# First-layer rotation tables of an S5 mixer made per quarter and kept on chip, with a new order of steps, in a two-layer hybrid decoder trunk

## The chip, the core and the metric

The kernel runs on one core of a Trainium2 chip. A core has a matrix engine (PE), a vector engine (DVE), an activation engine (ACT), a small general engine (POOL) and a queue engine (SP); each works through its own instructions in order, and they wait for each other through semaphores. Copies between the chip's memory (SBUF) and DRAM are DMAs, which SP, ACT or POOL issue. The metric is the device time of one execution in microseconds (us), as the median of several runs.

## The reference

Two layers; each has a mixer and a feed-forward part. What the change touches is the S5 group inside the mixer, cut here to its core:

```python
h = x * (1.0 + scale1) + shift1
u, q, k, v = jnp.split(h @ w_in[l], [D_SSM, D_SSM + D_ATT, D_SSM + 2 * D_ATT], axis=-1)
# s5_mixer(u): 32 groups of 16 channels, each drives 64 complex states
delta = jnp.exp(log_step)[:, None]
mag, ang = jnp.exp(lam_re * delta), lam_im * delta
lb_re, lb_im = mag * jnp.cos(ang), mag * jnp.sin(ang)
bu_re, bu_im = jnp.einsum('blgc,gpc->blgp', u32, bb_re), jnp.einsum('blgc,gpc->blgp', u32, bb_im)
# s_t = (lb_re + i lb_im) * s_{t-1} + bu_t, by associative_scan over 512 tokens
y = Re(C s) + d_skip * u32
y = gelu(y); y = y * sigmoid(y @ glu_w + glu_b)
att = diff_attention(rotary(q), rotary(k), v)      # 4 heads, 2 softmax maps each
mix = concat([y, att]) @ w_out[l]
x = layer_norm(ALPHA * x + (1 + gate1) * mix)
x = layer_norm(ALPHA * x + (1 + gate2) * ffn(x))   # SwiGLU, 1024 -> 2816 -> 1024
```

## The kernel before

Every large matmul is done three times on numbers split in two: `mm3` multiplies high by high, high by low and low by high part. So each unit of weights (128 x 1024 numbers, `wunit`) is loaded by SP into `wraw`, its high part `whi` is copied by ACT, and its low part `wlo` is subtracted on DVE. PE's matmuls of a unit wait for both.

**The first layer's mixer** is where everything has to be made while the first matmuls run. In order of PE's work: the S5 input projection (`ups`) and the values (`vps`) with the modulation columns being reduced on DVE (`mraw`: one 128 x 1024 load and one instruction each); then the projections to q and k of four heads (`qkps`), 96 matmuls a head, into which the S5 steps, the attention steps (`sps`, `po`) and more `mraw` columns are woven; then the S5 gate (`glups`) and the output projection (`ops`). After that comes the feed-forward part (`gps`, `dps`).

**S5 in chunks of 8 tokens, in four quarters** `q` of 8 groups each. For the layer, `s5_params` makes powers of the state's factor (`pw`) and the angle of 8 steps, split in two parts (`hi`, `lo`), in five parts on POOL or DVE (`OPT["par"]` says which part is on DVE). For each quarter:

- `s5_build`: tables `Gt` and `QT` (each six 128 x 512 instructions on DVE), the kernel inside a chunk `kps` (PE), copied by ACT to `ksb`, finished by DVE and written by a DMA to DRAM (`kd`), from where eight POOL DMAs bring it back in Toeplitz form (`M`); `QT` is transposed on PE (`qps`) to `Q`.
- `s5_rot`: cosine and sine of k times the angle, k = 0 to 63: eleven DVE instructions on 128 x 256, and two sines on ACT. Written to DRAM (`sC`) by two DMAs, later loaded back to `csl` by SP in `inp`.
- `inp`, `inT`, `scan`, `sout`: the quarter's inputs are transposed (`utp`), multiplied by `Q` (`vps` of line 589), rotated by the tables (`rp`), scanned along the chunks, rotated back, and multiplied by `M` and `Gt` (`yps`).

**Buffers.** `thl`, `cs`, `ns`, `ksb`, `ta`, `btmp`, `dt`, `gl` and others take turns in two buffers of one ring, `t5`. An instruction that writes a buffer waits until whatever used it two turns ago is over; for a buffer that a DMA reads, until that DMA has landed.

**What sets the order.** Each engine's instructions are put in a fixed order when the kernel is built. The hints come from a string per step of the first stage (`START`: `p` the next part of `s5_params`, `r` of the rope tables, `v` a unit for the values, `V` matmuls of it, `A` two `mraw` columns, `b` a build step) and from `PLAN`: due times, counted in steps of the projections, for the kinds `bld` (build), `s5`, `att`, `mod` (`mraw`), `pf` (weight unit) and `cs` (`s5_rot` of the next quarter).

Of the kernel before, what the change touches and what calls it, by code (L numbers as in the profile page):

```python
# [14 lines left out]
ALU = mybir.AluOpType  # L15
# [4 lines left out]
START = ['', '', '', 'v', 'ppvV', 'rpV', 'ApvvA', 'VAVVb']  # L20
LAG, LAG1 = 2, 1
PLAN = ({'bld': [1.264, 2.8128, 2.8128, 7.5302, 15.0069, 15.7908, 16.6324, 22.2347, 24.025, 24.025, 24.025, 31.5693, 31.8037, 32.6247, 36.6694, 39.8654, 39.8664, 44.4181, 55.2875, 55.2875], 's5': [2.4963, 13.7411167, 15.82, 17.6903, 17.9768, 17.9768, 28.1555, 32.3101, 33.8664, 33.8664, 41.8348, 41.8348, 41.8348, 44.9401, 56.3771, 61.9808, 63.9276, 74.4357, 74.4357, 74.9633], 'att': [32.6299, 32.6299, 32.6299, 34.4688, 34.4688, 37.9126, 37.9126, 37.9126, 38.4369, 42.2702, 48.2563, 48.2563, 48.2563, 48.2563, 53.3008, 55.2114, 55.2114, 55.2114, 62.4974, 64.6963, 65.1666, 65.1666, 66.8965, 69.8788, 69.8788, 69.8788, 69.8788, 69.8788, 72.9166, 73.1266492, 78.0578164, 79.4594, 84.4816, 84.4816, 84.4816, 84.4816, 84.4816, 85.7045, 86.611, 86.611, 86.611, 87.1372, 87.1372, 87.1372, 87.1372, 87.1372, 87.1372, 87.1372, 87.1372, 87.1372, 87.7613, 88.3711, 92.1141, 94.0138, 95.5657, 99.9], 'mod': [10.9986, 18.0979, 25.5229, 28.8809, 38.8480964, 39.702, 45.7126, 48.3167, 48.3167, 49.5891, 50.7771, 51.8893, 59.3159, 62.6235, 62.6235, 62.6235, 65.1638, 68.4286, 78.3464, 89.495], 'pf': [15.904, 15.9839, 26.2995, 26.2995, 39.217, 46.2033, 61.5805, 61.9828, 61.9828, 77.3237, 84.6088, 88.9481, 89.2859, 89.9011], 'cs': [2.3738, 2.3738, 3.9308, 15.3106]}, {'s5': [0, 9.5668, 14.1521, 22.5905, 23.0853, 23.0853, 28.7962, 33.7987, 53.4804, 53.9093, 54.6366, 54.6366, 54.6366, 54.89, 57.9461, 62.766, 63.1181, 64.2437, 76.6993, 79.0981], 'att': [32.001, 32.001001, 32.001001, 32.001001, 32.001001, 36.2691, 36.9654, 49.5504, 49.5634, 49.946, 52.2004, 52.2014, 52.2014, 53.123, 53.4199, 53.4634231, 53.4644231, 54.3593, 56.3216, 58.3250688, 61.5574297, 61.5584297, 62.6277, 62.6277, 64.4714996, 64.4715006, 64.4715016, 64.4715026, 64.4715036, 64.4715046, 64.4715056, 64.4715066, 64.4715076, 64.4715086, 64.4715096, 64.4715106, 64.4715116, 64.4715126, 82.7565, 82.7565, 82.7566, 82.7566, 83.9079, 87.4356, 87.4366, 87.4376, 90.018, 91.9921, 91.9931, 91.9941, 91.9951, 91.9951, 91.9951, 91.9951, 91.9951, 99.9], 'pf': [1.9638689, 9.1450603, 14.6524633, 14.6534633, 19.9457, 32.098, 37.9847, 48.098, 51.1731991, 74.7986995, 74.7986995, 81.1276, 84.5849, 86.8909]})
OPT = {'par': [0, 0, 1, 0, 0], 'MODQ': 'sync', 'q_bld': 1, 'q_s5': 0, 'q_att': 0, 'q_pf': 0, 'CSQ': 'scalar', 'plo': [[1, 0, 1, 0, 0, 0, 0, 0, 0, 0, 0, 1, 0, 0, 0, 0, 0, 0], [0, 0, 0, 0, 0, 0, 0, 1, 1, 0, 0, 0, 0, 1, 0, 0, 0, 0]]}
# [3 lines left out]
P = 128  # L27
# [35 lines left out]
def trunk_kernel(tc, xT, x, c, pos, modw, modb, wst, s5a, s5bc, s5d, glub, lamv, subw, lng, lnr, out):  # L63
    nc = tc.nc
    from contextlib import ExitStack

    with ExitStack() as es:
# [355 lines left out]
        def s5_build(l, q, pm):  # L423
# [54 lines left out]
            ksb = t5([P, P], name="ksb")  # L478
# [27 lines left out]
        def s5_rot(l, q, pm):  # L506
# [9 lines left out]
            cs = t5([P, 2, 4, 64], name="cs")  # L516
# [9 lines left out]

            ns = t5([P, 256], name="ns")
            ts(ns, flat(st), -1.0, ALU.mult)
            eng = getattr(nc, "gpsimd" if l else OPT["CSQ"])
            eng.dma_start(sC[q][:, 256:768], cs.rearrange("p r g k -> p (r g k)"))  # L530
            eng.dma_start(sC[q][:, 0:256], ns)
# [118 lines left out]
        def s5_gen(l, u2, us, yh, yl):  # L650
# [3 lines left out]
            def inp(q):  # L654
                if l:
                    Q[q] = s5_load_q(l, q, us[0][:, 0:1] if q == 0 else src)
                U[q] = s5_in(u2, q)
                C[q] = sm([P, 768], "csl", 1)
                nc.sync.dma_start(C[q], sC[q])
# [22 lines left out]
            seq = [(fn, (q,)) for q in range(4) for fn in (inp, inT, scan, sout)]  # L682
            seq += [(yT, (b, ih)) for b in range(2) for ih in range(2)]
# [259 lines left out]
        for l in range(L):  # L943
# [7 lines left out]
            if l == 0:  # L951
# [18 lines left out]
                rots = list(range(4))  # L970
# [16 lines left out]
                with queued(marks(), (POOL,)), strict():  # L987
# [5 lines left out]
                    for k in range(NK):  # L993
# [11 lines left out]
                        for c_ in START[k]:  # L1005
# [4 lines left out]
                            elif c_ == "c":  # L1010
                                s5_rot(0, rots.pop(0), pms[0])
                            elif c_ == "p":
                                next(par, None)
                            elif c_ == "r":
                                next(rope, None)
                            elif c_ == "b":
                                next(bld)
                            else:
                                mods_bg(cols, 2, "A2")
# [36 lines left out]
            def tick():  # L1056
                while plan and plan[0][0] < now[0] + 1:
# [10 lines left out]
                    elif kind == "cs":  # L1068
                        with queued(marks() if OPT["q_bld"] else m0, (POOL,)):
                            if rots:  # L1070
                                s5_rot(0, rots.pop(0), pms[0])
# [315 lines left out]
```

## Time and profile before

| | |
|---|---|
| time of the runs | median 1258.78 us of 3 (1256.43 to 1260.86) |
| the profiled execution | 1254.48 us, its span 1252.7 us |
| PE busy | 1186.2 us, 95% of the span |
| DVE busy | 813.6 us, 65% |
| ACT busy | 481.9 us, 38% |
| POOL busy | 162.3 us, 13% |

The span runs from the first to the last instruction; the 1.8 us around it are the same launch. Busy shares are averages over stages: after the first layer's mixer PE is busy nearly all the time, so what happens before that is what can be won or lost here.

### The profile page before, as it was taken

How to read it: one execution, taken by the hardware profiler on the slowest of the kernel's cores; microseconds unless marked ns; L12 is line 12 of the kernel's file. 1: busy time of each engine (PE TensorE's matmuls, PEld its weight loads, DVE VectorE, ACT ScalarE, POOL GpSimd, SP SyncE). 2: the span in 40 equal slices, each digit the busy share in tenths (PEclk: the TensorE clock that was granted, in tenths of full speed). 3: DMA queues.
4: the chain of work that ended last, by engine and by line, in shares of the span. 5: the costliest groups of instructions: out<-in, count | busy, mean ns of one | idle time of the engine just before them, and what ended most of it. 6: DMA issues, size and time to landing. Idle time of an engine off the chain costs nothing.

```text
span 1252.7 us, 17629 instructions
## 1 busy us (share of the span) xinstructions
PE 1186.2 (95%) x6736; PEld 988.7 (79%) x6736; DVE 813.6 (65%) x1505; ACT 481.9 (38%) x848; POOL 162.3 (13%) x289
## 2 busy tenths in 40 slices
PE   4898788999999999999999999999999999999997
PEld 3687676779888888888877788877988888888885
DVE  6779798786787675798558366757665222244556
ACT  3436255536222222343446355553623222234330
POOL 8921230010000010000001243000000000000001
PEclk9899789999999999999999999999999999999999
DMA  9784535535577577645334663223463333333241
GB/s 351 270 209 125 105 84 167 176 128 166 187 256 270 178 234 192 199 157 166 102 98 144 195 178 102 72 97 102 158 192 97 93 100 101 97 89 117 68 134 68
DMA packets 60469, 188.68 MB, mean 151 GB/s; under 512 B 8065, under 2 KB 13985, under 8 KB 60385
## 3 DMA queue, kind: packets, MB, share of 16 engines
q1 hardware_dynamic: 51408, 170.94, 43.0%
q0 software_dynamic: 5088, 13.42, 4.1%
q10 hardware_dynamic: 3888, 3.20, 1.0%
q8 instruction: 53, 0.87, 0.3%
q14 instruction: 32, 0.25, 0.1%
HBM read 172.90 MB, written 12.53 MB: 148 GB/s over the span
## 4 chain that ended last, share of the span: by engine, by line
PE 73%; DVE 11%; POOL 6%; DMA 4%; issue 4%; ACT 2%; DVEq 0%; POOLq 0%; ACTq 0%
PE gps L116 39%; PE dps L116 18%; PE ops L116 4%; PE qkps L116 2%; PE vps L116 2%; POOL s5tmp L104 1%; PE ups L116 1%; DVE wlo L104 1%; DMA wraw<-in_wst 1%; PE glups L116 1%; PE po L116 1%; DVE mraw L110 1%; DVE x L107 1%; PE sps L757 1%; DMA kd<-ksb 1%
## 5 line engine op out<-in xcount | busy, mean ns | idle before, releaser
L104 DVE TENSOR_TENSOR wlo<-wraw,whi 128x1024 fp32r<-128x1024 f32 x180 | 219.6, 1222 | 262.8 <-ACT whi L113 262.1
L113 ACT ACTIVATE whi<-wraw 128x1024 fp32r<-128x1024 f32 x184 | 194.2, 1057 | 390.3 <-PE gps L116 249.8
L116 PE MATMUL gps<-hT2h,whi 128*128 128x512 f32 (+1 forms) x768 | 286.5, 373 | 0.6 <-DVE rtmp L104 0.4
L116 PE MATMUL gps<-hT2l,whi 128*128 128x512 f32 (+1 forms) x768 | 285.8, 372 | 0.0
L116 PE MATMUL gps<-hT2h,wlo 128*128 128x512 f32 (+1 forms) x768 | 285.4, 372 | 0.0
L116 PE MATMUL dps<-whi,ah 128*128 128x512 f32 x704 | 219.6, 391 | 0.0
L116 PEld LDWEIGHTS gps<-hT2h,whi 128*128 128x128 f32 x768 | 144.7, 188 | 26.0 <-DVE rtmp L104 0.9
L116 PEld LDWEIGHTS gps<-hT2l,whi 128*128 128x128 f32 x768 | 144.7, 188 | 24.9
L116 PEld LDWEIGHTS gps<-hT2h,wlo 128*128 128x128 f32 x768 | 144.7, 188 | 24.9
L116 PEld LDWEIGHTS dps<-whi,ah 128*128 128x128 f32 x704 | 132.2, 188 | 28.6 <-DVE rtmp L104 1.2
L116 PE MATMUL dps<-wlo,ah 128*128 128x512 f32 x352 | 137.1, 390 | 0.0
L110 DVE SCALAR_TENSOR_TENSOR mraw<-mraw,scb 128x1024 f32<-128x1024 f32 x96 | 114.2, 1219 | 5.4 <-DMA mraw<-in_modw 5.4
L113 ACT ACTIVATE ah<-aT 128x512 fp32r<-128x512 f32 x88 | 53.6, 626 | 91.2 <-PE dps L116 72.8
L104 DVE TENSOR_TENSOR ah<-aT,ah 128x512 fp32r<-128x512 f32 x88 | 59.3, 688 | 41.3 <-ACT ah L113 41.1
L116 PEld LDWEIGHTS dps<-wlo,ah 128*128 128x128 f32 x352 | 66.1, 188 | 13.4
L116 PE MATMUL ops<-whi,am 128*128 128x512 f32 x128 | 43.1, 398 | 0.0
L761 ACT ACTIVATE e<-sps,nm 128x128 f32<-128x128 f32 (+3 forms) x64 | 33.3, 525 | 19.3 <-DVE nm L759 18.7
L554 POOL DMA_DIRECT2D M<-kd x64 | 33.8, 535 | 41.0 <-DMA kd<-ksb 37.9
L116 PE MATMUL qkps<-wlo,hTh 128*128 128x256 f32 x128 | 38.1, 298 | 0.5 <-DVE wlo L104 0.5
L116 PE MATMUL qkps<-whi,hTh 128*128 128x256 f32 x128 | 37.9, 298 | 0.0
L116 PE MATMUL qkps<-whi,hTl 128*128 128x256 f32 x128 | 37.9, 297 | 0.0
L116 PE MATMUL qkps<-whi,hTnh 128*128 128x256 f32 x128 | 37.4, 293 | 0.0
(285 smaller groups left out, 1858.9 us busy)
## 6 DMA issues: line engine op xcount, KB each, us to landing
wraw<-in_wst SPq DMA_DIRECT2D x184, 512.0 KB, 3.7
mraw<-in_modw SPq DMA_DIRECT2D x96, 512.0 KB, 5.1
M<-kd POOLq DMA_DIRECT2D x64, 64.0 KB, 4.4
gb<-in_lnr SPq DMA_DIRECT2D x8, 512.0 KB, 3.9
csl<-sC SPq DMA_DIRECT2D x8, 384.0 KB, 3.7
xT<-in_xT SPq DMA_DIRECT2D x8, 256.0 KB, 6.7
x<-in_x SPq DMA_DIRECT2D x4, 512.0 KB, 4.6
G<-gd SPq DMA_DIRECT2D x4, 512.0 KB, 4.8
```

The lines of the kernel that those rows point to most:

```text
L104: (eng or nc.vector).tensor_tensor(out, a, b, op=op)
L107: nc.vector.scalar_tensor_tensor(out, a, s, b, op0=op0, op1=op1)
L110: nc.vector.scalar_tensor_tensor(out, a, s, b, op0=ALU.mult, op1=ALU.mult, accum_out=acc_out)
L113: nc.scalar.activation(out, in_, AF.Copy, scale=scale)
L116: nc.tensor.matmul(ps, a, b, start=start, stop=stop)
L554: nc.gpsimd.dma_start(M[16 * j : 16 * j + 16], ksrc)
L757: nc.tensor.matmul(ps[:, m, c_], qT[rows, i * P : (i + 1) * P], kT[rows, c_], start=False, stop=c_.stop == n)
L761: nc.scalar.activation(e[:, m, :n], ps[:, m, :n], AF.Exp, bias=nm[:, m : m + 1], accum_out=ss[:, i, m : m + 1])
```

## The change

The rotation tables of the first layer are no longer written to DRAM and read back. `s5_rot` makes them into a tile `tri` of one buffer, which `scan` reads; the next quarter's tables are made after the scan that read the last ones. `ksb` gets a buffer of its own too. In the second layer the tables still go through DRAM, with one DMA in place of two. `START` and `PLAN` have new entries, kind `cs` is gone, and part 3 of `s5_params` (five small instructions: the cosine's two, and three for the power of 8 of the magnitude, `r8`) is on DVE in place of POOL.

```diff
-START = ['', '', '', 'v', 'ppvV', 'rpV', 'ApvvA', 'VAVVb']
+START = ['', '', '', 'v', 'pvrpVp', '', 'pVVAvv', 'AAVbV']
...
-            ksb = t5([P, P], name="ksb")
+            ksb = sm([P, P], "ksb", 1)
...
-            cs = t5([P, 2, 4, 64], name="cs")
+
+            tri = sm([P, 768], "tri", 1)
+            cs = tri[:, 256:].rearrange("p (r g k) -> p r g k", r=2, g=4)
...
-            ns = t5([P, 256], name="ns")
-            ts(ns, flat(st), -1.0, ALU.mult)
-            eng = getattr(nc, "gpsimd" if l else OPT["CSQ"])
-            eng.dma_start(sC[q][:, 256:768], cs.rearrange("p r g k -> p (r g k)"))
-            eng.dma_start(sC[q][:, 0:256], ns)
+            ts(tri[:, 0:256], flat(st), -1.0, ALU.mult)
+            if l:
+                nc.gpsimd.dma_start(sC[q], tri)
+            return tri
...
-                C[q] = sm([P, 768], "csl", 1)
-                nc.sync.dma_start(C[q], sC[q])
+                if l:
+                    C[q] = sm([P, 768], "tri", 1)
+                    nc.sync.dma_start(C[q], sC[q])
+
+            def rot(q):
+                C[q] = s5_rot(0, q, pms[0])
...
             seq = [(fn, (q,)) for q in range(4) for fn in (inp, inT, scan, sout)]
+            if l == 0:
+
+                seq = [(rot, (0,))] + [(fn, (q + (fn is rot),)) for q in range(4) for fn in (inp, inT, scan, rot, sout)
+                                       if fn is not rot or q < 3]
```

How the instructions move, at three places. The names are tiles of the program; a number in a name is the buffer's.

**ACT, end of the first stage.** Before: `whi_357` is the high part of a unit for the values, `s5tmp` the sine of the S5 angle, `xT_330` the input of the seventh and eighth step.

```order
L113 ACTIVATE whi_326<-wraw_324 128x1024
L370 ACT_TABLE_LOAD
L370 ACTIVATE s5tmp_143<-s5tmp_143 128x16
L371 ACTIVATE s5tmp_143<-s5tmp_143 128x16
L113 ACTIVATE whi_357<-wraw_355 128x1024
L980 ACTIVATE xT_330<-xT_330,mods_114 128x512
```

After: the same unit is `whi_355`.

```order
L113 ACTIVATE whi_326<-wraw_324 128x1024
L113 ACTIVATE whi_355<-wraw_353 128x1024
L226 ACT_TABLE_LOAD
L226 ACTIVATE rcos_121<-rang_152 128x32
L227 ACTIVATE rsin_122<-rang_152 128x32
L370 ACTIVATE s5tmp_143<-s5tmp_143 128x16
L371 ACTIVATE s5tmp_143<-s5tmp_143 128x16
L987 ACTIVATE xT_330<-xT_330,mods_114 128x512
```

The unit's high part now stands ahead of the sines and of the table load that they need.

**DVE, the third quarter's `QT`.** Before, `ksb` is followed by the `QT` table, whose temporaries `ta` take turns with `ksb` in the ring.

```order
L107 SCALAR_TENSOR_TENSOR ksb<-mask_86,s5dt,ksb 128x16
L104 TENSOR_TENSOR QT<-pw,s5bc 128x512
L104 TENSOR_TENSOR ta<-pw,s5bc 128x512
L104 TENSOR_TENSOR QT<-pw,s5bc 128x512
L104 TENSOR_TENSOR QT<-QT,ta 128x512
L104 TENSOR_TENSOR ta<-pw,s5bc 128x512
L110 SCALAR_TENSOR_TENSOR mraw,mods<-mraw,scb 128x1024
L104 TENSOR_TENSOR QT<-QT,ta 128x512
L107 SCALAR_TENSOR_TENSOR gl<-gl,yps 128x512
```

After:

```order
L107 SCALAR_TENSOR_TENSOR ksb<-mask_86,s5dt,ksb 128x16
L104 TENSOR_TENSOR QT<-pw,s5bc 128x512
L104 TENSOR_TENSOR ta<-pw,s5bc 128x512
L104 TENSOR_TENSOR QT<-pw,s5bc 128x512
L104 TENSOR_TENSOR QT<-QT,ta 128x512
L104 TENSOR_TENSOR ta<-pw,s5bc 128x512
L772 RECIPROCAL rho<-ss 128x1 x2
L104 TENSOR_TENSOR QT<-QT,ta 128x512
```

The order is nearly the same; what differs is that `ksb` is no longer in the ring that `ta` takes its buffer from.

**PE, the first head's projection.** Here only the change is shown: after 24 of the head's 96 matmuls (`qkps`; `hTh_135` belongs to the second of its two weight units) come the first quarter's transposes and products and the second quarter's `kps`. Before, the head's 96 matmuls and 23 of the next ran without them.

```order
L116 MATMUL qkps<-whi,hTh_135 128x256 x2
L495 MATMUL qps<-ident,QT 128x128 x4
L575 MATMUL utp<-ident,UU 128x128 x4
L495 MATMUL qps<-ident,QT 128x128 x4
L589 MATMUL vps<-UU,Q 64x64 x16
L476 MATMUL kps<-Gt,s5bc 32x112 x8
L476 MATMUL kps<-s5bc 32x16 x8
L116 MATMUL qkps<-wlo,hTh_135 128x256
```

And DVE between that head's two weight units: the second one's low part (the last row) follows the first quarter's `QT`, two `mraw` columns, the second quarter's whole `Gt` (its last rows here) and the first quarter's first rotation (`rp`, `wz`).

```order
L104 TENSOR_TENSOR Gt<-pw,s5bc 128x4x128
L104 TENSOR_TENSOR s5bc<-btmp 128x64 x2
L104 TENSOR_TENSOR ta<-pw,s5bc 128x512
L445 COPY s5bc<-s5bc 64x8x16 x2
L104 TENSOR_TENSOR Gt<-Gt,ta 128x4x128
L104 TENSOR_TENSOR Gt<-pw,s5bc 128x4x128
L104 TENSOR_TENSOR ta<-pw,s5bc 128x512
L104 TENSOR_TENSOR rp<-vps,tri 128x1024
L104 TENSOR_TENSOR Gt<-Gt,ta 128x4x128
L104 TENSOR_TENSOR wz<-rp 128x512
L104 TENSOR_TENSOR wlo<-wraw,whi 128x1024 x2
```

Before, eleven instructions of the second `s5_rot` and the lambda's small ones stood between the two units.

## Rows read from the trace of the kernel before

**Rows 1.** Stretches: us, busy PE, PEld, DVE, ACT, POOL; PEclk, DMA share, GB/s.

```profile
62.60:101.00 38.40, 34.97 (x265) 31.39 (x264) 30.59 (x73) 15.15 (x25) 10.22 (x19) 1.00 0.85 211
101.00:149.00 48.00, 37.06 (x391) 31.51 (x391) 46.74 (x102) 22.36 (x51) 11.20 (x18) 0.86 0.41 100
157.00:215.00 58.00, 47.60 (x444) 39.52 (x443) 52.39 (x118) 30.03 (x80) 11.12 (x23) 0.91 0.44 127
270.00:1252.70 982.70, 964.66 (x5147) 804.45 (x5146) 596.84 (x1055) 362.95 (x598) 71.72 (x126) 1.00 0.45 142
```

**Rows 2.** The same view, three stretches at half of the granted clock.

```profile
44.40:51.20 6.80, 6.08 (x14) 4.85 (x15) 5.00 (x8) 4.53 (x8) 6.35 (x13) 0.51 0.87 310
133.20:146.80 13.60, 10.27 (x102) 8.58 (x103) 13.23 (x31) 3.79 (x7) 3.00 (x5) 0.50 0.21 7
160.50:167.30 6.80, 5.74 (x28) 5.77 (x28) 5.16 (x13) 3.78 (x9) 1.16 (x4) 0.50 0.43 115
```

**Rows 3.** What PE waited for, 14 to 215 us: total, times, longest.

```profile
PE qps L495 <- DVE QT L104: 5.6, 2, 3.9
PE qps L495 <- DVE gl L107: 4.5, 1, 4.5
PE vps L116 <- ACT whi L113: 4.1, 1, 4.1
```

**Rows 4.** What DVE waited for, 60 to 215 us.

```profile
DVE ksb L107 <- ACT ksb L113: 2.0, 2, 1.8
DVE thl L104 <- DMA sC<-ns: 1.0, 1, 1.0
```

**Rows 5.** ACT in order of time: start, us, instruction, idle before and releaser.

```profile
37.48 1.28 ACT L370 ACT_TABLE_LOAD   x1
43.80 0.21 ACT L370 ACTIVATE s5tmp<-s5tmp 128x16 f32<-128x16 f32 x1 [5.04 <-POOL s5tmp L101]
44.03 1.04 ACT L113 ACTIVATE whi<-wraw 128x1024 fp32r<-128x1024 f32 x1
```

**Rows 6.** DMAs that SP issued from 36.7 to 36.85 us: to landing.

```profile
wraw<-in_wst SPq DMA_DIRECT2D x1, 512.0 KB, 3.9
```

**Rows 7.** POOL in order of time, while DVE works and after.

```profile
52.72 2.22 POOL L104 TENSOR_TENSOR pt<-pw 128x16 f32<-128x16 f32 x2
58.80 0.45 POOL L104 TENSOR_TENSOR pt<-pw 128x32 f32<-128x32 f32 x2
```

**Rows 8.** DVE in order of time.

```profile
62.63 0.31 DVE L104 TENSOR_TENSOR btmp<-s5bc,kre 128x128 f32<-128x128 f32 x1 [4.03 <-POOL pw L104]
67.83 0.41 DVE L104 TENSOR_TENSOR thl<-kio,phihi 128x256 f32<-128x256 f32 x1
75.67 0.43 DVE L104 TENSOR_TENSOR thl<-kio,phihi 128x256 f32<-128x256 f32 x1
156.41 0.69 DVE L104 TENSOR_TENSOR ta<-pw,s5bc 128x512 f32<-128x512 f32 x1 [7.15 <-DMA kd<-ksb]
157.02 1.22 DVE L110 SCALAR_TENSOR_TENSOR mraw<-mraw,scb 128x1024 f32<-128x1024 f32 x1
```

**Rows 9.** DMAs issued from 140.9 to 157 us: count, size, us to landing.

```profile
mraw<-in_modw SPq DMA_DIRECT2D x1, 512.0 KB, 10.9
csl<-sC SPq DMA_DIRECT2D x1, 384.0 KB, 10.0
kd<-ksb ACTq DMA_DIRECT2D x1, 64.0 KB, 9.5
gd<-mods POOLq DMA_DIRECT2D x1, 4.0 KB
```

**Rows 10.** The chain that ended last, in order of time: start, us, count.

```profile
75.23 0.88 PE qkps L116 x7
```

**Rows 11.** ACT in order of time, a change from one function to another.

```profile
106.04 1.28 ACT L226 ACT_TABLE_LOAD   x1
107.34 0.42 ACT L226 ACTIVATE cs<-thl 128x256 f32<-128x256 f32 x1
```

More of the change, by code (lines that the diff above doesn't have):

```diff
@@ L23 @@
-OPT = {'par': [0, 0, 1, 0, 0], 'MODQ': 'sync', 'q_bld': 1, 'q_s5': 0, 'q_att': 0, 'q_pf': 0, 'CSQ': 'scalar', 'plo': [[1, 0, 1, 0, 0, 0, 0, 0, 0, 0, 0, 1, 0, 0, 0, 0, 0, 0], [0, 0, 0, 0, 0, 0, 0, 1, 1, 0, 0, 0, 0, 1, 0, 0, 0, 0]]}
+PLAN = ({'bld': [1.264, 9.7422, 9.7422, 9.7422, 14.9651, 15.749, 16.5906, 22.1929, 22.1929, 22.1929, 24.025, 37.2093, 37.2093, 37.2093, 37.2093, 37.5556, 37.5556, 37.6922, 47.2335, 51.2975], 's5': [2.4963, 2.4963, 13.7411167, 15.7549, 16.3159, 17.3447, 17.6312, 17.6312, 27.5389, 29.1309, 32.0391, 33.5954, 33.5954, 41.5638, 41.5638, 42.0266, 42.0266, 44.7445, 56.1815, 61.7852, 61.7852, 69.5125, 75.5358, 76.4414], 'att': [35.1225, 35.1225, 35.1225, 35.1225, 39.086, 42.5298, 42.5298, 42.5298, 51.7938, 51.7938, 51.7938, 51.7938, 51.7938, 51.7938, 51.7938, 54.4569, 54.627, 54.9951, 62.2811, 64.48, 64.9503, 64.9503, 66.6802, 69.6625, 69.6625, 69.6625, 78.4397, 78.4397, 79.837, 79.837, 79.837, 80.0583, 82.8643, 83.6832, 83.6832, 83.6832, 83.6832, 83.6832, 83.6832, 83.6835, 85.8594, 86.182, 86.182, 86.182, 86.4646, 86.4646, 87.2019, 87.2019, 89.8545, 90.0201, 90.0201, 90.0201, 91.7712, 93.6709, 94.4899, 99.9], 'mod': [10.9986, 18.0979, 25.4081, 29.1177, 38.4565, 39.561, 46.2652, 50.2857, 56.5072, 56.5072, 56.5072, 56.6114, 59.2761, 67.3515, 68.5094, 70.1035, 71.3002, 71.7973, 77.5725, 87.4454], 'pf': [15.904, 15.9839, 25.6408, 27.5246, 39.1909, 41.8561, 52.834, 55.2905, 55.7125, 71.3859, 85.832, 89.8625, 90.5091, 90.5218]}, {'s5': [0, 9.5668, 14.1521, 22.5905, 23.0853, 23.0853, 28.7962, 33.7987, 53.4804, 53.9093, 54.6366, 54.6366, 54.6366, 54.89, 57.9461, 62.766, 63.1181, 64.2437, 76.6993, 79.0981], 'att': [32.001, 32.001001, 32.001001, 32.001001, 32.001001, 36.2691, 36.9654, 49.5504, 49.5634, 49.946, 52.2004, 52.2014, 52.2014, 53.123, 53.4199, 53.4634231, 53.4644231, 54.3593, 56.3216, 58.3250688, 61.5574297, 61.5584297, 62.6277, 62.6277, 64.4714996, 64.4715006, 64.4715016, 64.4715026, 64.4715036, 64.4715046, 64.4715056, 64.4715066, 64.4715076, 64.4715086, 64.4715096, 64.4715106, 64.4715116, 64.4715126, 82.7565, 82.7565, 82.7566, 82.7566, 83.9079, 87.4356, 87.4366, 87.4376, 90.018, 91.9921, 91.9931, 91.9941, 91.9951, 91.9951, 91.9951, 91.9951, 91.9951, 99.9], 'pf': [1.9638689, 9.1450603, 14.6524633, 14.6534633, 19.9457, 32.098, 37.9847, 48.098, 51.1731991, 74.7986995, 74.7986995, 81.1276, 84.5849, 86.8909]})
@@ L24 @@
+OPT = {'par': [0, 0, 0, 1, 0], 'MODQ': 'sync', 'q_bld': 1, 'q_s5': 0, 'q_att': 0, 'q_pf': 0, 'CSQ': 'scalar', 'plo': [[1, 0, 1, 0, 0, 0, 0, 0, 0, 0, 0, 1, 0, 0, 0, 0, 0, 0], [0, 0, 0, 0, 0, 0, 0, 1, 1, 0, 0, 0, 0, 1, 0, 0, 0, 0]]}
 NOSYNC = mybir.DependencyInfo(mybir.DependencyClass.NoSync, mybir.DependencyReason.DATA)
@@ L969, in trunk_kernel @@
                 cols += [(0, j) for j in range(16, 40)]
-                rots = list(range(4))
                 def first_x(k):
@@ L1009, in trunk_kernel @@
                                 first_v()
-                            elif c_ == "c":
-                                s5_rot(0, rots.pop(0), pms[0])
                             elif c_ == "p":
@@ L1067, in tick @@
                             prefetch(wb + pfs.pop(0))
[L1068 to L1071, printed above, removed]
                     elif kind == "bld":
```

1 line of the change is left out of this document (removed).

## The prediction

> **What bounds the kernel now.** I read the stretches by engine first. From 270 us on PE is busy for 964.66 of 982.7 us at full granted clock [rows 1]. There only less work for PE would save time, and the change gives PE the same matmuls, so the tail (with the second layer, whose tables now take one DMA of POOL in place of two) is costed at nothing: DVE has 597 of 983 us of work there and POOL 72, so a wait of a few us on either is covered, and 18 us of PE's idle time in the whole tail is the most that could come of it. The first layer's mixer is the other case. Of 106 us in the stretches 101 to 149 and 157 to 215, PE is idle 10.94 and 10.40, together 21.3, and DVE is busy 46.74 of 48 and 52.39 of 58 [rows 1]. There DVE is the bound: it makes the tables, the low parts and the rotations, and PE waits for it. From 62.6 to 101 it isn't: DVE has 30.59 of 38.4 us.
>
> Second I read what each waits for. PE's longest waits are one of 4.1 us for ACT's `whi`, one of 4.5 for DVE's `gl` and two of together 5.6 for `QT` [rows 3]. Third, the granted clock: 0.51 from 44.4 to 51.2, 0.50 from 133.2 to 146.8 and from 160.5 to 167.3, which is the lower of TensorE's two levels, 1.2 GHz [rows 2]. The first of these lies around the start of PE's matmuls on the unit whose `whi` ends at 45.07 [rows 5], behind the wait of 4.1. A stretch of 6.8 us at half clock does 3.4 us of full-clock work, so such a wait costs up to 3.4 us more than its length, where PE is what counts.
>
> Last I read DVE's own stalls. At 156.41 it starts `ta` after 7.15 us in which it did nothing, released by the DMA `kd<-ksb` [rows 8]. `ta` wanted the ring's buffer that `ksb` had, and that DMA, 64 KB, took 9.5 us to land. It was not alone: the `mraw` column's 512 KB took 10.9 us and the 384 KB of `csl` 10.0, all issued beside `gd<-mods`, a transfer of 4 KB on POOL's queue [rows 9]. An earlier 512 KB for `wraw` took 3.9 [rows 6].
>
> **The change, part by part.** Negative is time saved.
>
> *A. The first stage's order on ACT, and part 3 off POOL.* Before, ACT loads a table at 37.48, then stands 5.04 us for POOL's `s5tmp`, and `whi` behind it starts at 44.03 and takes 1.04 [rows 5]. Its `wraw`, issued at about 36.8, landed 3.9 later, at 40.7 [rows 6]. Now `whi` is ahead of the load, so it can end at 41.75 in place of 45.07: 3.3 us earlier. What is queued behind it now waits (sines, then the powers), and those end at `pw`, for which DVE's `btmp` at 62.63 idled 4.03 us [rows 8]: this is the wait that sets the end of the stage, so the moved `whi` alone gives nothing there. What helps is POOL: five small instructions leave it. An instruction of POOL's takes 0.22 us while DVE is quiet and 1.11 beside a busy DVE (0.45 and 2.22 for two) [rows 7]. Five are 1.1 us at the first price and 5.5 at the second, of which no more than 3.3 can count, because PE's first stage gains no more. Bounds -1.1 and -3.3; I take **-2.0**, about the middle.
>
> *B. `ksb` in its own buffer.* `ta` no longer waits for `kd`: at most **-7.1**, since DVE is the bound here. The lower bound is 0: the next `mraw` instruction, at 157.02 [rows 8], needs a load that was issued beside `kd` and landed no sooner (10.9 us [rows 9]), and would stall in its place. In the new order two `mraw` columns and the build stand earlier, and the loads wanted next are issued ahead of `gd`. So I take the whole of it. `ksb`'s buffer is now waited for by the next quarter's `ksb` alone, a whole quarter later, with 9.5 us to be covered.
>
> *C. No round trip of the tables.* Gone are DVE's waits of 1.0 for `sC<-ns` and, for `ksb`, of 2.0 (longest 1.8), for ACT's copy of `kps`, on whose queue the table DMAs are issued [rows 4]: **-2.8** for the longest of each, 0 if other waits take their place. The `csl` loads ran ahead of their use and are costed at nothing; if that cover were gone, one takes 10.0 us [rows 9]. A single buffer for the tables means that the rotation of the next quarter can't begin before the scan that reads the last. That is DVE's own order (rotation behind scan), so no wait is added, except for the sines of ACT between them.
>
> *D. Moved work.* The three later rotations, eleven instructions each, leave 62.6 to 101, where DVE has 7.8 us to spare, for 101 to 215, where it has little. `thl` of the first and second stand at 67.83 and 75.67 [rows 8], 7.8 us apart with a `wlo` and other work between, so three rotations are no more than 23.5 us. Builds go the other way: a `Gt` is the 5.2 us from `btmp` at 62.63 to 67.83. With a `QT` at 0.6 us for an instruction (156.41 to 157.02 [rows 8]), 3.7 for six, one build is 8.9. Two to three builds take the place of three rotations, so the moves cancel and I put **0**.
>
> *E. New waits.* By hand from `pw` at 60.6: `Gt` of the first quarter to 65.8, the rotation and `wlo` to 73.6 (7.8 more), `QT` to 77.3, two `mraw` columns at 1.22 [rows 8] to 79.8, the second `Gt` with one `rp` of 1.2 to 86.2, `wz` and `wlo` to about 88. PE comes to its transposes of `QT`, after 24 matmuls of the first head, at about 75, waits 2.5, then 5.4 for the second `Gt` and 1.1 for `wlo`: some 9 us in which it did nothing. The head's other 70 `qkps`, at 0.125 us (0.88 for seven [rows 10]), end at 97, or at 100.4 with half clock behind the wait. DVE has work of its own to 97 or so and then stands 0 to 3.3 us for q and k of that head. As DVE is the bound, only this counts: **+2**.
>
> *F. Two more table loads.* In the new order sines stand between the exponentials four times, and the mixer has six loads where it had four. One takes 1.28 us and the next activation starts 0.02 us behind it (106.04 to 107.34) [rows 11]. Two are 2.6, the upper bound; ACT is busy 22.36 of 48 us and 30.03 of 58 [rows 1], so half or less is seen by DVE: **+1.3**, lower bound 0.
>
> Here the Trainium skill speaks against the change: "ScalarE: Activation LUTs", section "Rules for kernel authors", has all functions of one table set grouped before a switch, and "What ACT_TABLE_LOAD costs" puts a switch at 1283 ns and about 1380 ns of drain, together some 2.66 us. The trace agrees with the first figure and shows no drain behind it, so the measurement decides. By the page's figure F would be an estimated 5.3 and the sum -4.6, a median of 1254.2.
>
> **Sum.** -2.0 - 7.1 - 2.8 + 0 + 2.0 + 1.3 = -8.6. The profiled execution took 1254.5 us (1252.7 its span), so 1245.9 for one like it. It lay 4.3 under the median of the runs, 1258.8, which the same 8.6 takes to **1250.2**. The bounds add up to -13.2 and to +4.8 (A -1.1, B and C 0, E 3.3, F 2.6).
>
> **Rivals.** *The hold-up only moves (no change).* Loads beside `gd` took some 10 us whatever their size, 64 to 512 KB [rows 9]. If `gd` still meets loads that DVE wants next, B is 0 and the sum -1.5: 1257.3. For it speaks that the next `mraw` landed no sooner than `kd`; against it, that in the new order the columns end earlier, and `gd` with them. It would also come out so if another user of the ring waited as `ta` did.
>
> *PE becomes the bound of the mixer (slower).* Then E's new waits count in full: 9, and 3.4 for half clock behind them, less the 3.3 of `whi` and the 4.5 of the wait for `gl` [rows 3], which the earlier builds would spare: +4.6, 1263.4. It decides if PE's 21.3 us of idle time from 101 to 215 do not shrink; they have to give back more than the 9 + 3.4 - 3.3 = 9.1 that are new, so that about 12 remain, and at 17 or more the change is lost. Against it: DVE, not PE, is full there now [rows 1].
>
> **How the numbers follow.** I give the forecast 0.62, the moved hold-up 0.22 and the bound on PE 0.16. About 0.3%, 3.8 us, is what can be told from no change here. Within the forecast I see 1242 to 1255: the lower end is the bound of -13.2 and one half-clock stretch (3.4) that falls away. Some of its upper part (0.03) is within 0.3%, some of the moved hold-up (0.04) is faster, and some of the bound on PE (0.02) ends within 0.3%: so faster 0.63, same 0.23, slower 0.14. The range 1242 to 1261 leaves out the dearest part of the last rival.
>
> **What the changed profile would show.** A: `whi` at about 41, `pw` at about 60.6, no wait of 4.1 for `whi`. B: no wait of DVE for `kd`, and `gd` with no load beside it that DVE wants. C: no `sC` in the first layer. D and E: PE idle about 9 us between 74 and 88, half clock after, and less idle time from 101 to 215. F: six loads, with DVE waiting for a sine less than 2.6 us in all. I'm wrong if the mixer ends no sooner though `ta` doesn't stall: then the time has gone to a load that waits, or to PE.

## The result, and the profile after

The changed kernel took 1242.62 us (median of 4 runs, 1241.61 to 1244.35), the kernel before in the same comparison 1257.63 (4 runs). The ratio is 0.9878, 95% interval 0.9854 to 0.9902; a second comparison gave 0.986 (0.984 to 0.9879). So it is 15 to 17.6 us faster, where 8.6 were forecast. The two profiled executions lie closer together: 1254.48 and 1243.17 us, spans 1252.7 and 1241.4, a difference of 11.3.

Where this comes from shows in the time at which PE reaches the same matmuls. These are rows of the view by tile of the kernel before (ns min/median/max; first and last start in us; forms):

```profile
L116 PE MATMUL qkps<-whi,hTh x128: 277/283/562, 75.0 to 198.9; 128*128 128x256 f32 x128
L116 PE MATMUL glups<-yh,whi x16: 388/392/792, 206.2 to 225.1; 128*128 128x512 f32 x16
L116 PE MATMUL gps<-hT2h,whi x35: 279/283/385, 285.2 to 299.8; 128*128 128x256 f32 x35
```

and of the changed kernel:

```profile
L116 PE MATMUL qkps<-whi,hTh x128: 277/283/416, 70.1 to 188.3; 128*128 128x256 f32 x128
L116 PE MATMUL glups<-yh,whi x16: 387/395/501, 191.7 to 215.9; 128*128 128x512 f32 x16
L116 PE MATMUL gps<-hT2h,whi x67: 278/283/396, 272.8 to 299.8; 128*128 128x256 f32 x64, 128*128 128x512 f32 x3
```

PE is 4.9 us ahead at the first projection to q and k, 14.5 at the S5 gate and 12.4 at the first feed-forward matmul; 1.1 of it is gone by the end. In a second pair of profiles (runs `before_again` and `after_again`, below) it is 4.8, 13.8 and 16.3 us ahead at these places, and 16.3 at the end. The stretches of the changed kernel (columns as in [rows 1], the first three answer to rows there):

```profile
62.60:101.00 38.40, 31.36 (x264) 27.22 (x262) 32.02 (x71) 12.51 (x21) 8.77 (x19) 0.78 0.60 182
101.00:149.00 48.00, 45.29 (x483) 40.26 (x481) 45.95 (x103) 26.89 (x56) 10.54 (x21) 0.96 0.29 70
157.00:215.00 58.00, 51.75 (x421) 41.14 (x419) 54.55 (x124) 37.74 (x97) 6.11 (x12) 1.00 0.47 144
74.00:88.30 14.30, 7.53 (x85) 5.67 (x83) 13.44 (x26) 3.57 (x5) 5.87 (x12) 0.60 0.35 91
76.50:93.00 16.50, 11.21 (x98) 9.77 (x99) 15.61 (x29) 3.32 (x5) 5.47 (x13) 0.51 0.50 146
```

The new order pays first: PE's idle time from 62.6 to 101 goes from 3.4 to 7.0, and 16.5 us run at half clock there. It wins later: from 101 to 149 and 157 to 215 PE is idle 8.96 us in place of 21.3, and the granted clock is 0.96 and 1.00 in place of 0.86 and 0.91. DVE has 45.95 and 54.55 us of work there, as full as ever.

What DVE waited for from 62 to 101 us, in the changed kernel (us in all, times, longest):

```profile
DVE rot L104 <- ACT qkt L113: 2.1, 1, 2.1
DVE tri L104 <- ACT tri L226: 1.0, 2, 0.5
DVE ksb L107 <- ACT ksb L113: 0.7, 1, 0.7
```

From 101 to 149 it waited for ACT's `gl` alone, 1.8 us. The wait for `kd` and the one for the tables' DMA [rows 4, 8] are gone, and no DMA has taken their place between 62 and 215 us.

Two sums are used below for the profiled execution of each kernel, over the part from the first `qkps` to the first `gps`, worked out from stretches of 1.7 us of the windows view: *idle* is their length less PE's busy time, and *lost at half clock* is PE's busy time times (1 - granted clock). Before: 26.0 idle and 9.6 lost. After: 19.1 and 7.7.

### The profile page after: what moved, and what is told of

It reads as the page before. It is cut to its first block, busy times and chain, and to the rows that moved or that the text cites. A ratio compares the mean times of both kernels' runs of the same rounds, so it can differ in the third digit from the quotient of the medians.

```text
span 1241.4 us, 17579 instructions
## 1 busy us (share of the span) xinstructions
PE 1185.0 (95%) x6736; PEld 986.9 (80%) x6736; DVE 814.3 (66%) x1510; ACT 484.1 (39%) x850; POOL 163.5 (13%) x280
## 4 chain that ended last, share of the span: by engine, by line
PE 74%; DVE 10%; POOL 5%; issue 4%; DMA 4%; ACT 3%; DVEq 0%; POOLq 0%; ACTq 0%
PE gps L116 38%; PE dps L116 18%; PE ops L116 4%; PE qkps L116 3%; DMA mraw<-in_modw 2%; PE vps L116 2%; DMA wraw<-in_wst 1%; PE yps L629 1%; POOL s5tmp L104 1%; PE glups L116 1%; PE ups L116 1%; DVE mraw L110 1%; PE po L116 1%; DVE x L107 1%; DVE QT L104 1%
## 5 line engine op out<-in xcount | busy, mean ns | idle before, releaser
L769 ACT ACTIVATE e<-sps,nm 128x128 f32<-128x128 f32 (+3 forms) x64 | 33.3, 526 | 17.7 <-DVE nm L767 17.6
```

The lines of the kernel that those rows point to most:

```text
L769: nc.scalar.activation(e[:, m, :n], ps[:, m, :n], AF.Exp, bias=nm[:, m : m + 1], accum_out=ss[:, i, m : m + 1])
```

## Experiments

Ratios are to the kernel before, run on the same chip; "us" is the difference of two ratios times 1257. The order of instructions is made anew for each kernel, so an edit also makes instructions change places. Behind each edit stands therefore how many lines DVE's order differs by from that of the kernel that was edited (alike neighbours are one line, and a line that moved counts twice).

### The parts one by one in the old order

**`ksb` in its own buffer, alone** (76 lines): of the change's edits the line that makes `ksb`, which is the same code for both layers.

> The kernel before with one edit: `ksb` in a buffer of its own. Theory 1 (the gains lie in waits that were removed, each on its own: the first stage about 5 us, the wait for `kd<-ksb` about 7): the 7.1 us stall of `ta` is gone and no other takes its place, so 5 to 7 us faster, ratio 0.9945 to 0.996. Theory 2 (DVE is full, and a single wait removed is filled by the next one; the gain comes from the new order of the mixer with the tables on chip): `mraw` waits in place of `ta`, no more than 2 us faster, ratio 0.998 to 1.000.

Ratio 1.0032 (1.0008 to 1.0055): 4 us slower. Both theories missed the sign. The stall for `kd` is gone, and other waits stand there. From its view of waits of DVE, 56 to 230 us:

```profile
DVE yl L104 <- ACT yh L113: 5.9, 2, 5.1
DVE mraw L110 <- DMA mraw<-in_modw: 4.9, 1, 4.9
DVE ta L104 <- DMA sC<-ns: 3.9, 1, 3.9
```

`mraw` waits for the load issued beside `gd`, as the rival of the moved hold-up had it. (The wait for `yl` is in the kernel before too, 2.0 us in one execution and 5.0 in the other.) And `ta` waits 3.9 us for the tables' DMA: with `ksb` out of the ring the turns shift, and `ta` gets the buffer of `ns`, which a DMA reads too. These waits don't show where the 4 us are lost. In this execution, 3.45 us above the median of its runs, the first `gps` comes at 287.8 us, between the two executions of the kernel before (285.2 and 288.9). Behind it 975.2 us pass in place of 967.5: at 587 us PE waits 4.5 us for `Q` of the second layer and then runs at half clock. Why `Q` is late there stays open.

**The new first stage alone** (6 lines).

This is the change's new `START`, and in `OPT` (cut here) part 3 of `s5_params` on DVE:

```diff
-OPT = {'par': [0, 0, 1, 0, 0], ...
+OPT = {'par': [0, 0, 0, 1, 0], ...
```

> The kernel before with the new first stage alone: the new `START` and the part of `s5_params` that goes to DVE. Theory 1: PE's wait of 4.1 us for `whi` and the stretch of half clock from 44 to 51 us go, and `Gt` of the first quarter starts some 3.4 us earlier; the first `qkps` comes about 5 us earlier and the end 4 to 5 us, ratio 0.996. Theory 2: PE comes 5 us earlier to a mixer in which DVE is the bound and DVE gains only 1.4 us (the last `pw` at 61.2 in place of 62.6): no more than 2 us faster, ratio 0.998 to 1.000.

Ratio 0.996 (0.9944 to 0.9977), 5 us faster: theory 1. The first `qkps` came at 72.4, the first `gps` at 280.6, 4.6 earlier.

**Both of these**: the two edits together (80 lines).

> The kernel before with both of the last two edits: `ksb` in its own buffer and the new first stage; the rotation tables still go through DRAM and the mixer's order is the old one. Theory 1: the two add up, 9 to 12 us faster, ratio 0.990 to 0.993, most of the whole change. Theory 2: 0 to 4 us faster, ratio 0.997 to 1.000; the rest of the whole change's 15 us is the order and the tables.

Ratio 1.0025 (1.0002 to 1.0048). Neither theory: the two don't add up to a gain, and the 5 us of the first stage are lost beside `ksb`. DVE waits for `mraw` 4.2 and for `sC<-ns` 4.1 in this kernel as well. Its profiled execution, 1253.05 us, is near the lowest of its twelve (1252.77 to 1267.53), so the trace doesn't show where the median loses.

### The parts undone in the new order

**`ksb` back in the ring** (148 lines): the line that makes `ksb` as it was, in the changed kernel.

> The changed kernel with one edit undone: `ksb` takes turns again in the ring of two buffers with `ta` and the others. Theory 1: if a DMA of `kd` is slow in this order too, `ta` stalls again, and 5 to 7 us of the change's 15 are lost, ratio 0.992 to 0.994 to the kernel before. Theory 2: in the new order `kd` lands in 3.7 us and `ta` waits 0 to 2 us: ratio 0.987 to 0.989, as the changed kernel.

Ratio 0.9966 (0.9951 to 0.9982): 11 to 13 us of the gain are lost, more than the whole stall of the kernel before and more than either theory had. The stall for `kd` itself is short, 2.3 us, so most of the loss is not this wait. Idle is 23.3 and lost at half clock 11.6, 8.1 more together than in the changed kernel.

**The old first stage** (6 lines): `START` and `OPT` as they were, in the changed kernel.

> The changed kernel with the old first stage (old `START`, part 3 of `s5_params` on POOL again); all else as in the change, and the order on PE and DVE moves by a few rows only. Theory 1 (the first stage is worth what it was worth in the old mixer, 4.1 us): 3 to 5 us slower than the changed kernel, ratio 0.990 to 0.992. Theory 2 (in the new order PE waits for `QT` and `Gt` in the first head anyway, so an earlier PE only waits longer there): 1 to 2 us slower, ratio 0.988 to 0.990.

Ratio 0.989 (0.987 to 0.991), 1.5 to 4 us slower by the two comparisons of the changed kernel; its interval overlaps with both of theirs. PE's wait of 4.1 us for `whi` is back and the first `qkps` comes at 73.5, 3.4 later; at the gate PE is 0.6 ahead of the changed kernel (191.1 to 191.7). The two theories aren't told apart by the time, but the trace shows where the 3.4 go: from the first `qkps` to the gate it takes 117.6 us in place of 121.6, with 3.3 lost at half clock there in place of 7.7. PE is idle as long in both, 15.5 and 15.4 us to the gate, and from 70 to 100 us it waits for `Gt` and `QT` alike (2.0 and 1.8 to 1.9 us). So the earlier PE didn't wait longer, as theory 2 had it: in this pair of executions what it gained went into half clock.

**The tables' trip through DRAM put back** (173 lines), into the one buffer `tri`:

```diff
-            if l:
-                nc.gpsimd.dma_start(sC[q], tri)
+            (nc.gpsimd if l else nc.scalar).dma_start(sC[q], tri)
+            if l == 0:
+                nc.sync.dma_start(tri, sC[q])
             return tri
```

> The changed kernel with the tables' trip put back: each quarter's table is written to DRAM by a DMA of ACT's queue and loaded by SP into the same buffer before the scan reads it. Theory 1 (what the tables on chip give is the end of DMA waits): the first scan waits the whole trip, 5 to 8 us, the later ones 0 to 3 each: 5 to 10 us slower than the changed kernel, ratio 0.992 to 0.996. Theory 2 (the trip is hidden behind the builds): no more than 2 us slower, ratio 0.987 to 0.990.

Ratio 0.9935 (0.9912 to 0.9959), 7 to 9 us slower than the changed kernel. This is theory 1's size but not its mechanism: no scan waits for the trip. DVE waits for `mraw` in its place (62 to 230 us), where the changed kernel has no such wait, and SP waits for the tables' writes before it can issue the loads back (60 to 215 us):

```profile
DVE mraw L110 <- DMA mraw<-in_modw: 5.4, 6, 3.3
SPq L531 <- DMA sC<-tri: 9.5, 4, 4.0
```

The column for which DVE stands 3.3 us was issued at 103.99 us, as the third behind such a load (102.67), and landed 9.6 us later. Idle is 21.4 and lost 11.2, 5.8 more together. How much of the 7 to 9 us comes from the added DMAs, and how much from the 173 lines of DVE's order, this run doesn't separate.

### The hold-up of the loads

**The gate columns written in rows.** The columns of each gate (two in each layer, `gate1` and `gate2`) go to DRAM as `gd` and come back as `G`. In this edit PE transposes the eight columns, ACT copies them, and `gd` is written as 8 rows of 512 bytes in place of 1024 single numbers (22 lines in the kernel before, 28 in the changed one).

```diff
-            nc.gpsimd.dma_start(gd.rearrange("k p -> p k"), mods[:, l, 24 * w + 16 : 24 * w + 24])
+            gps = ps5("gps8")
+            nc.tensor.transpose(gps[0:NK, 0:P], mods[:, l, 24 * w + 16 : 24 * w + 24], ident)
+            gsb = t2([NK, P], name="gsb")
+            cp(gsb, gps[0:NK, 0:P])
+            nc.gpsimd.dma_start(gd, gsb)
```

In the kernel before:

> The kernel before with one edit: the eight gate columns are transposed on PE and copied by ACT, so that `gd` is written as 8 rows of 512 bytes in place of 1024 single numbers. Theory 1 (the single numbers hold up the loads beside them): `kd`, `mraw` and `csl` land in 3 to 5 us in place of 10, the stall of `ta` shrinks to 0 to 2 us, and the kernel is 4 to 7 us faster, ratio 0.9945 to 0.997. Theory 2 (they are slow for another reason): the landings stay at 8 us or more and the time within 2 us, ratio 0.998 to 1.002.

In the changed kernel:

> The changed kernel with the same edit of `gd`. Theory 1: nothing that DVE wants stands beside `gd` in the new order, so within 2 us of the changed kernel, ratio 0.986 to 0.990. Rival: later `gd`s or the first one still hold loads up, and 3 us or more come off, ratio 0.985 or less.

Ratios 1.0005 (0.9989 to 1.0021) and 0.9942 (0.9922 to 0.9962): by their times neither kernel is in the range of theory 1, and the changed one is 8 us slower, which its rival missed too. In both the mixer did what theory 1 said: the first feed-forward `gps` came at 278.4 in place of 285.2, and at 271.9 in place of 272.8. But the spans came out at 1253.2 and 1246.2: 7.3 and 5.7 us were given back behind it. The traces show where. In both, `gd` of the two feed-forward gates is written too late: DVE's `rtmp` waits for `G<-gd` twice, 13.5 and 13.8 us in all. PE waits 1.8 and 1.7 us for `rtmp`, and from DVE's last instruction to the end of the span 4.9 and 4.2 us more pass than without the edit. What the end waits for, the profile doesn't show. So:

**In rows for the first gate alone**, the later ones as they were (12 lines in either kernel), by a condition `l == 0 and w == 0` on the same edit.

> The kernel before, with the gate columns transposed on PE for the first layer's first gate alone; the three later gates as they were. In the run that had all four transposed the first feed-forward matmul came at 278.4 in place of 285.2 us, and the end did not follow. Theory 1 (the hold-up by single numbers is worth 6 to 7 us in the first mixer, and the three later transposes took it back by stopping PE): 5 to 7 us faster than before, ratio 0.9945 to 0.996. Theory 2 (the mixer's gain is lost later whatever the other gates do): within 2 us of before, ratio 0.998 to 1.002.

> The changed kernel with the same edit for the first gate alone. Theory 1: the changed kernel's loads are not held up where DVE wants them, so 0 to 2 us faster than the changed kernel, ratio 0.986 to 0.989 to the kernel before. Theory 2: as for all four gates, 5 us slower than the changed kernel, ratio 0.992 to 0.994.

The kernel before gets 0.9941 (0.9925 to 0.9957), 7.4 us faster, in the range of theory 1. The loads issued from 141 to 157 us in it (size, us to landing), to be held against [rows 9]:

```profile
mraw<-in_modw SPq DMA_DIRECT2D x2, 512.0 KB, 5.3
csl<-sC SPq DMA_DIRECT2D x1, 384.0 KB, 3.1
kd<-ksb ACTq DMA_DIRECT2D x1, 64.0 KB, 2.4
```

10.9, 10.0 and 9.5 have become 5.3 (the first of the two 4.0), 3.1 and 2.4: the 4 KB of `gd` held them up. The edit does more than write rows, though. The rows come by way of PE and ACT, and POOL issues them 85 us later. From POOL in order of time, the kernel before and then this run:

```profile
140.99 0.91 POOL L313 DMA_DIRECT2D gd<-mods  x1 [3.84 <-DVE qkt L104]
225.92 0.58 POOL L318 DMA_DIRECT2D gd<-gsb  x1 [1.03 <-ACT gsb L113]
```

So beside these loads there was no `gd` at all. That the single numbers do it shows elsewhere. Beside the last gate's `gd` in the kernel before, issued at 945.1 us (the window from 945 to 953 us):

```profile
wraw<-in_wst SPq DMA_DIRECT2D x2, 512.0 KB, 9.5
gd<-mods POOLq DMA_DIRECT2D x1, 4.0 KB, 11.3
```

and beside the rows (this run, 225.9 to 227 us):

```profile
wraw<-in_wst SPq DMA_DIRECT2D x1, 512.0 KB, 4.2
gd<-gsb POOLq DMA_DIRECT2D x1, 4.0 KB, 2.3
```

The changed kernel gets 0.9874 (0.9851 to 0.9897), not told apart from itself, as theory 1 said: its own `gd` is issued at 119.7, takes 8.8 us, and no other DMA is issued beside it from 119.5 to 129.9 us. None of the versions that were tried is clearly faster than the changed kernel.

**`ksb` in its own buffer and the first gate in rows**, in the kernel before.

> The kernel before with `ksb` in its own buffer, and the first gate's `gd` written in rows. Theory 1 (`ksb` alone lost because the hold-up by `gd` moved on to `mraw` and to the tables' DMAs): without the hold-up it is as fast as `gd` in rows alone or faster, ratio 0.990 to 0.995. Theory 2 (taking `ksb` out of the ring is bad for the old order by itself, since the other users change turns): slower than `gd` in rows alone by 3 us or more, ratio 0.997 or more.

Ratio 0.9989 (0.9967 to 1.0012), 6 us slower than the gate in rows alone: theory 2. `mraw` doesn't wait any more, `ta` still waits 3.6 us for `sC<-ns`. So the moved hold-up is not all of what `ksb` alone cost. The rest lies in the changed turns of the ring or in the instructions that changed places with them; no run separates the two.

### What a stall of DVE costs

**Extra work on DVE** in the changed kernel, ahead of the `QT` of the third quarter (n = 1, 4 or 12 instructions of 0.6 us; 89, 96 and 108 lines), or of the fourth (n = 4; 99 lines). The values are overwritten by the next instruction.

```diff
+            for _ in range(n if l == 0 and q == 2 else 0):
+                tt(m8(qt[:, 1]), pwb(0, 1), vb(bbi), ALU.mult)
             cpart(qt[:, 1], pwb(0, 1), vb(bbi), pwb(1, 1), vb(bbr), ALU.add)
```

> The changed kernel with four more DVE instructions of 128 x 512 (2.4 us) ahead of the third quarter's `QT`, where the kernel before stalled for `kd`; they write values that are overwritten. This measures what a stall of DVE there costs by itself. Theory 1 (DVE is the bound, and a stall costs its length): 2.4 us slower than the changed kernel, ratio 0.989 to 0.9905. Theory 2 (a stall of DVE makes PE wait and brings a stretch of half clock with it, so it costs more than its length): 4 us or more, ratio 0.991 or more. Theory 3 (there is slack): 0 to 1 us, ratio 0.9875 to 0.9885.

> The same with twelve more instructions (7.2 us, as long as the stall for `kd` in the kernel before). Theory 1: 7.2 us slower than the changed kernel, ratio 0.993 to 0.994. Theory 2: 9 us or more, ratio 0.995 or more. Theory 3: 0 to 4 us, ratio 0.988 to 0.991.

> The changed kernel with one extra DVE instruction of 128 x 512 (0.6 us) ahead of the third quarter's `QT`; the order on PE and DVE changes in nearly the same rows as with four. Theory 1 (the stall costs more than its length, by waits of PE and half clock): 0 to 3 us slower than the changed kernel, ratio 0.988 to 0.990. Theory 2 (the rows that changed places cost the 5 us or more, not the stall): 5 us or more slower, ratio 0.992 or more.

> The changed kernel with four extra DVE instructions (2.4 us) ahead of the fourth quarter's `QT` in place of the third's. Theory 1 (DVE is full in the whole mixer and a stall costs more than its length wherever it is): 4 to 10 us slower than the changed kernel, ratio 0.991 to 0.996. Theory 2 (only the third quarter is that tight): 0 to 2.5 us slower, ratio 0.988 to 0.990.

| extra work | ratio | 95% interval | idle | lost at half clock |
|---|---|---|---|---|
| none | 0.9878, 0.986 | | 19.1 | 7.7 |
| 0.6 us | 0.9927 | 0.9899 to 0.9955 | 19.6 | 9.3 |
| 2.4 us | 0.9958 | 0.994 to 0.9977 | 22.3 | 14.1 |
| 7.2 us | 1.0039 | 1.0015 to 1.0063 | 26.2 | 16.3 |
| 2.4 us, fourth quarter | 0.9947 | 0.9927 to 0.9966 | 23.2 | 12.2 |

The runs with 2.4 and 7.2 us came out in the range of "costs more than its length", but the one with 0.6 us shows that this reading is too simple. Its 0.6 us cost 6 to 8 us; that is theory 2 of its run: most of it is the instructions that changed places, not the 0.6 us. From there the three lie near a line: 3.9 us more for 1.8, 10.2 more for 4.8. Over the outer two a microsecond of DVE costs 2.1, by their intervals 1.4 to 2.8; but their orders differ by 114 lines, so this slope may hold a cost of the order too. The first two differ by only 17 lines; their slope is 2.2, and their intervals overlap, so that it isn't clear of one or of nothing. That a stall of DVE costs twice its length is thus likely here and not shown. Half of the extra shows as PE idle and half as half clock: from 0.6 to 7.2 us of extra work idle grows by 6.6 and the lost part by 7.0. From the run with 7.2, where the kernel before had its stall and behind it:

```profile
149.00:157.00 8.00, 5.11 (x30) 4.20 (x34) 7.60 (x17) 2.05 (x5) 0.00 (x0) 0.59 0.09 36
157.00:215.00 58.00, 47.99 (x421) 37.95 (x413) 47.65 (x105) 29.19 (x73) 7.35 (x16) 0.85 0.42 129
```

The granted clock is 0.59 and 0.85, where the changed kernel has 1.00 in either.

**One step moved**: the second quarter's `kps`, for which PE waited 2.0 us, is due four steps later (169 lines).

```diff
-... 14.9651, 15.749, 16.5906, 22.1929, ...
+... 14.9651, 15.749, 20.5, 22.1929, ...
```

> The changed kernel with one due time changed: the second quarter's `kps` (PE waited 2.0 us there for `Gt`) comes four steps later in the first head. Theory 1 (PE's waits in the first head are covered, since DVE is the bound): within 2 us of the changed kernel, ratio 0.986 to 0.990. Theory 2 (each wait of PE ahead of a stretch of half clock counts): 2 to 4 us faster, ratio 0.984 to 0.986. Rival (the changed places on DVE cost more): slower, ratio 0.991 or more.

Ratio 1.0005 (0.9988 to 1.0022), 16 to 18 us slower than the changed kernel: the rival, and far beyond its size. One due time, with no buffer and no table touched, takes the whole gain. PE waits 6.2 us for `qkt`, 5.5 for `wz` and 3.7 for `wlo`, all on DVE, which has other work ahead of them; idle is 30.7 and lost 13.0.

### Both kernels once more

> The kernel before, unchanged, profiled a second time. Theory 1 (its spread lies in the hold-up in the first mixer): if this execution takes 1257 us or more, the stall of `ta` and the stretches of half clock in the mixer are longer than in the first profile (7.1 us; 9.6 us of PE work lost to half clock from the first `qkps` on). Theory 2 (the spread lies in the feed-forward part): the first feed-forward matmul comes within 1 us of 285.2 and the rest is longer.

> The changed kernel, unchanged, timed against the kernel before in five rounds. By the forecast's sum, 8.6 us: ratio 0.9932. By the pair of profiled executions, 11.3 us: 0.991. By the medians of the first comparison, 15.0: 0.988.

The changed kernel again: 0.986 (0.984 to 0.9879), a little more gain than the largest of the three expected. Its profiled execution, 1242.49, lies 2.7 above the median of its four runs. The kernel before took 1259.01 us in this execution, 4.5 more than in the first profile. Its stall for `kd` was shorter, 6.3 us, so that half of theory 1 falls; the half clock is what differs. At the S5 gate, in the second execution:

```profile
203.00:218.00 15.00, 14.13 (x45) 9.46 (x46) 9.04 (x21) 4.93 (x16) 0.00 (x0) 0.50 0.35 111
```

and in the first:

```profile
205.00:208.60 3.60, 3.55 (x15) 2.71 (x14) 3.42 (x11) 2.62 (x11) 0.00 (x0) 0.54 0.26 105
209.00:224.00 15.00, 13.75 (x70) 10.39 (x69) 12.90 (x25) 6.84 (x16) 0.00 (x0) 1.00 0.57 172
```

PE's waits just ahead are alike, 1.07 us for `gl` and 1.83 or 1.94 for `rho`. Behind them one execution ran some 4 us at half clock, the other more than 15. The first `gps` came at 288.9 in place of 285.2.

The other traces say the same. From the first `glups` to the first `gps`, by stretches of 1 us, PE lost at half clock:

| order | traces | lost, us |
|---|---|---|
| old (the kernel before, and three edits of it) | 4 | 0.6 to 1.1 |
| old (the kernel before a second time, and three edits of it) | 4 | 6.7 to 6.9 |
| new (the changed kernel twice: 0.0) | 12 | 0.0 to 1.7 |

And of the 107 executions of the kernel before that were timed beside the other kernels (median 1257.7), the 42 with a mean granted clock of 0.983 or more took 1255.2 us on average, the 26 with 0.979 or less 1259.8.

## Why the prediction was right in its sign and half its size

**The step from the profiled execution to the median failed.** It said that the execution "lay 4.3 under the median of the runs, 1258.8, which the same 8.6 takes to 1250.2". The 4.3 were taken for a constant that the change leaves alone. They are not, for a term is missing from the sum: the half clock at the S5 gate. In the old order PE loses some 1 us or some 7 us to it; the first profile was of the short kind, and the changed kernel loses 0.0 in both of its profiles. There PE has no wait over 0.9 us from 186 to 200 us, the granted clock is 1.00 from 157 to 215, and the first profiled execution lies 0.6 above its median. For one execution like the profiled one the forecast was 1245.9, and 1243.17 came: 2.7 of the miss of 7.6 are the sum's, the rest is this step. Against the second pair of profiles (1259.01 and 1242.49) the gain is 16.5.

**A was mis-sized.** It was held to -3.3 at most and taken as -2.0; PE was 4.9 us ahead at the first `qkps`. PE's wait for `whi` fell from 4.1 to 0.9 us, and the half clock from 44 to 51 [rows 2] went with it (the granted clock of that stretch is 1.00 now), a term that had been read and left out of the sum. `whi` started at 40.70 as worked out, and the last `pw` ended at 61.2 in place of 60.6. In the old order the stage is worth 5 us at the end; in the new order 1.5 to 4, not clear of nothing.

**B came near the price of the hold-up by luck.** With `gd` out of the way the old kernel is 7.4 us faster, and 7.1 were forecast; but that edit frees the loads of `mraw` and of the tables too, and it leaves `ksb` in the ring. The change's own edit is worth 7.1 in neither order: alone in the old order it makes the kernel 4 us slower, and undone in the new order it costs 11 to 13. So "at most -7.1, since DVE is the bound here" is not a bound. The rival of the moved hold-up was right about the old order (`mraw` waits 4.9) and wrong about the new one: there `gd` is issued 21 us earlier, with no load beside it, and moving it away gains nothing.

**C's size stays open.** The waits that it named are gone or shorter: none for `sC`, and 0.7 us for `ksb` where the longest was 1.8. The trip put back costs 7 to 9 us and not 2.8; DVE doesn't wait for it there, but for `mraw`, whose loads stand behind the trip's in SP's queue. What the sum didn't see is that the tables' DMA and `kd` read buffers of one ring: taking out `ksb` alone makes `ta` wait for `ns` (3.6 to 4.1 us in the three runs with `ksb` out and the tables in), and only with both out does nothing in the ring wait for a DMA. That this makes B and C worth more together is argued from these waits; no run took the tables alone out of the ring.

**D, E and F.** D, put at 0, was not measured by itself. E stood: DVE's wait for q and k of the first head is 2.1 us (+2.0 taken). PE's wait there, forecast as some 9 us, is 14.3 - 7.53 = 6.8 us from 74 to 88.3; the half clock behind it was forecast as one stretch of 6.8 us and lasts 16.5 (the stretches above). For F, DVE waited 1.0 us for the tables' sines from 62 to 101 and 1.8 for ACT's `gl` from 101 to 149; together that is 2.8, inside the bounds of 0 to 2.6 only if not all of `gl` is a table load's. The rival that PE becomes the bound did not come: its idle time in these stretches fell from 21.3 to 8.96, below the 12 named as even.

The new table loads are as cheap as the old. ACT of the changed kernel, in order of time:

```profile
103.67 1.28 ACT L636 ACT_TABLE_LOAD   x1
104.97 0.63 ACT L636 ACTIVATE gl<-gl 128x512 f32<-128x512 f32 x1
```

The load takes 1.28 us and the activation starts 0.02 us behind it. The drain that the Trainium skill adds in "ScalarE: Activation LUTs" ("What ACT_TABLE_LOAD costs") doesn't show here either.

**What stays open.** The parts undone one by one cost 11 to 13, 7 to 9 and 1.5 to 4 us, more than the 15 to 17.6 of the whole, so no split of the gain over the parts is right. Every edit of the changed kernel that changed DVE's order by 89 lines or more cost 6 us or more, whatever it was meant to do; the two with 6 and 12 lines cost 4 at most and nothing (the one with 28 lost most of its 8 us to the later gates). So a rival stands: that the new order itself, with its due times, is the gain, and that any other order loses it. How much of what undoing `ksb` or the tables costs is the wait, and how much the instructions that changed places with it, these runs don't separate; the new order with both undone was not run. What is shown is where the gain lies: in PE's idle time and half clock up to the first feed-forward matmul.

## What to carry to other kernels

Price a stall on the engine that feeds PE with what the clock loses behind it: here, from 0.6 to 7.2 us of extra work on DVE, PE's idle time and the half clock grew alike. Take the median, not one execution, as the start of a sum, and ask which of its waits are followed by half clock of varying length. When buffers share a ring, look at which users a DMA reads: taking one of them out shifts the turns, and may only hand the wait to the next. Where an edit makes the order of instructions anew, count what changed places before putting the time to the edit.

## What the runs showed of the hardware

A DMA of 4 KB in single numbers holds up loads on other queues: beside `gd` 64 to 512 KB landed after 9.5 to 10.9 us, without it after 2.4 to 5.3, and beside `gd` in rows a load of 512 KB landed after 4.2. The Trainium skill, "DMA: Bandwidth & Descriptors", section "Specifications", gives 512 bytes as the least size for full rate, and the trace agrees for `gd` itself (8.8 us for 4 KB in single numbers in the changed kernel, 2.3 in rows of 512 bytes); that others are slowed beside it is this case's finding.

The same waits of PE (1.07 and 1.8 to 1.9 us) were followed by some 4 us of half clock in one execution and by more than 15 in another. Nothing between was seen: in eight traces of the old order PE lost 0.6 to 1.1 us there, or 6.7 to 6.9.
